# First FFN of a hybrid decoder layer: input sums on VectorE in their own buffers, block weights fetched from the outset, plain weights in program order

## The chip, the cores and the metric

The kernel runs on one core of a Trainium2 chip. The metric is the device time of one execution in microseconds; a quoted time is the median of several executions. One more execution was taken with the hardware profiler, and every row of a trace comes from that one. In the rows PE is TensorE's matmul stream, DVE is VectorE, ACT is ScalarE, POOL is GpSimd, and SP is SyncE, which here issues DMAs and nothing else.

## The reference

One layer: a SwiGLU half step and a norm, three token mixers merged through gates, a second SwiGLU half step. The change concerns the first SwiGLU's input product.

```python
def swiglu_ffn(x, w_in, w_out):
    a, u = jnp.split(x @ w_in, 2, axis=-1)
    return (jax.nn.silu(a) * u) @ w_out

x = layer_norm(DEEPNORM_ALPHA * x + 0.5 * swiglu_ffn(x, ffn1_w_in[l], ffn1_w_out[l]), ln1_g[l], ln1_b[l])
mix = hybrid_mixer(x, mem, w_in[l], t5_table, ...)
x = layer_norm(DEEPNORM_ALPHA * x + mix, ln2_g[l], ln2_b[l])
x = layer_norm(DEEPNORM_ALPHA * x + 0.5 * swiglu_ffn(x, ffn2_w_in[l], ffn2_w_out[l]), ln3_g[l], ln3_b[l])
```

There are 512 tokens, 1024 channels and 2816 hidden units, all in float32.

## The kernel before

**Precision.** A float32 operand is split into a high part, rounded to the matmul's own float32 type by ScalarE (line 57), and a low part, the remainder, made by VectorE (line 58, a `tensor_tensor` with two inputs in SBUF). A product of two operands is three matmuls: high by high, low by high, high by low (`mm3`, lines 76 to 78). So a weight tile is usable when its DMA, then ScalarE, then VectorE have done their part, and the third matmul of the three is the one that needs VectorE's.

**The first FFN.** The hidden units are worked through in 22 blocks `j` of 128, each with two weight slabs of 128x1024, one for `a`, one for `u`. `gate` (line 128) takes SiLU of the first product on ScalarE (line 130) and multiplies by the second on VectorE (line 131). Blocks 0 to 2 are *plain*: 48 matmuls of 512 columns each, 144 in all. Blocks 3 to 21 are *seven-product* blocks: `x` is cut into four quarters (256 tokens by 512 channels), four sums of quarters `s1` to `s4` are split once and for all, and every block then needs seven quarter products of 12 matmuls of 256 columns (line 204), with the weights' own sums made on VectorE (lines 189 to 193).

**The opening.** `bring` (line 358) fetches `x` in five pieces and splits it; `first` calls it between the pieces of block 0's weights (line 150), and block 0's matmuls go channel block by channel block, `k` 0 to 7. `x` lands in `raws`, which take the two buffers `kv0` and `kv1`. The same two buffers hold the raw weights of the seven-product blocks (`s_raw`, line 176, DMAs of lines 177 and 178), so these can't be fetched until the sums are finished. `x_sums` (line 105) makes the four sums in place on GpSimd (lines 109 to 112) and splits them.

**What sets the order.** The scheduler places instructions of equal priority as they are written; everything under `tc.high_priority()` is placed ahead. Before, block 0's fetch, all plain weights (`weight`, line 65) and all block weights stand under it. There are three raw weight buffers (`w_raw`), which a later tile takes when the former has been split. All DMAs are issued by SP in one order, and a DMA that has to wait for a buffer holds up those behind it. The completion of a DMA is signalled on one of eight semaphores used in turn; in the listings they stand as DMAHW0 to DMAHW7, and an issue that reuses one waits for the transfer that had it.

Of the kernel before, what the change touches and what calls it, by code (L numbers as in the profile page):

```python
# [42 lines left out]
def hybrid_layer(ctx: ExitStack, tc: tile.TileContext, a: dict, out: bass.AP):  # L43
# [72 lines left out]
    def sum_tiles(pool):  # L116

        made = {n: [pool.tile([P, 4, 256], F32R, tag=f"s{n}{x}", name=f"s{n}{x}") for x in "hl"] for n in (3, 2, 1, 4)}
        return [made[n] for n in (1, 2, 3, 4)]

    def ffn_in(xT, w_in, gpool, kvp, pool, plain, sums=None, first=None, then=None):

# [14 lines left out]

        done = 0
        if first is not None:
            po = [ps("mm"), ps("mm")]  # L140
            with tc.high_priority():
                w = [weight_tiles() for _ in range(2)]
                steps = ((0, 1), (1, 2), (2, 4), (4, 6), (6, 8))
                for k0, k1 in steps:
                    c = slice(k0 * P, k1 * P)
                    r = slice((k0 % 4) * P, (k0 % 4 + k1 - k0) * P)
                    first(k0, k1)
                    for n in range(2):
                        raw, hi, lo = w[n]
                        nc.sync.dma_start(raw[:, c], slab(w_in, 0, n)[k0 // 4][:, r])  # L150
                        split(hi[:, c], lo[:, c], raw[:, c])
# [4 lines left out]
            then()
            done = 1
        else:
            opened = [([ps("mm"), ps("mm")], [weight(*slab(w_in, j, n)) for n in range(2)]) for j in range(2)]
# [729 lines left out]
```

## Time and profile before

| | |
|---|---|
| median of 3 runs | 1264.58 us (1264.14 to 1264.92) |
| the profiled execution | 1264.7 us, of which the span from first to last instruction is 1262.9 us |
| PE busy | 1241.3 us, 98% of the span |
| VectorE busy | 715.6 us, 57% |
| ScalarE busy | 474.1 us, 38% |
| GpSimd busy | 106.6 us, 8% |
| mean granted TensorE clock | 0.996 |

PE is the engine that sets the time: where it doesn't start a matmul, or starts them at half the rate, the program gets longer by that much. So the reading looks for the stretches where PE waits or runs slowly, and for what ended each wait.

### The profile page before, as it was taken

The numbers are of one execution on the slowest core, as the hardware profiler recorded it, in microseconds if no ns is written. First come the engines' busy times: TensorE is split into PE (matmuls) and PEld (weight loads), VectorE is DVE, ScalarE is ACT, GpSimd is POOL, SyncE is SP. The second block draws the span as 40 slices with busy tenths as digits, with TensorE's granted clock in tenths as the row PEclk, the third lists the DMA queues.
The fourth block names the chain that finished last, engine by engine and source line by source line (L and its number), as shares of the span: only waits on it lengthen the run. The fifth ranks groups of instructions, "written<-read, shape, count | busy, mean of one in ns | idle before, by whom it ended". The sixth has DMA issues, their size and how long they took to land.

```text
span 1262.9 us, 16539 instructions
## 1 busy us (share of the span) xinstructions
PE 1241.3 (98%) x6499; PEld 1053.2 (83%) x6499; DVE 715.6 (57%) x1146; ACT 474.1 (38%) x748; POOL 106.6 (8%) x91
## 2 busy tenths in 40 slices
PE   7999999999999999999999999999999999999997
PEld 5899999988888887788877877888988888888886
DVE  6788888643396899972554544435732222223336
ACT  5355555532235533523444532321332222222221
POOL 3000000000000000010321331120000000000003
PEclk9999999999999999999999999999999999999999
DMA  5333334543357233223333233233433322335312
GB/s 168 119 115 101 101 101 134 164 170 100 100 174 247 70 100 92 90 70 115 100 94 99 76 100 124 93 100 117 137 114 100 100 95 91 99 100 166 89 45 100
DMA packets 50926, 141.24 MB, mean 112 GB/s; under 512 B 6008, under 2 KB 7416, under 8 KB 50848
## 3 DMA queue, kind: packets, MB, share of 16 engines
q1 hardware_dynamic: 50848, 140.18, 34.8%
q8 instruction: 51, 0.84, 0.3%
q14 instruction: 27, 0.22, 0.1%
HBM read 132.80 MB, written 8.93 MB: 112 GB/s over the span
## 4 chain that ended last, share of the span: by engine, by line
PE 84%; DVE 9%; DMA 3%; issue 1%; ACT 1%; POOL 1%; SPq 0%; DVEq 0%; POOLq 0%; ACTq 0%
PE ps_mm L76 13%; PE ps_mm L77 13%; PE ps_mm L78 13%; PE ps_mm L204 8%; PE ps_ax L204 6%; PE ps_mm L251 4%; PE ps_mm L250 4%; PE ps_mm L249 4%; PE ps_ax L251 3%; PE ps_ax L250 3%; PE ps_ax L249 3%; DVE w_lo L58 2%; DMA w_raw<-in_ffn_w_in 1%; DVE mask L557 1%; PE ps_mm L350 1%
## 5 line engine op out<-in xcount | busy, mean ns | idle before, releaser
L58 DVE TENSOR_TENSOR w_lo<-w_raw,w_hi 128x1024 fp32r<-128x1024 f32 (+2 forms) x187 | 229.0, 1229 | 212.7 <-ACT w_hi L57 209.9
L57 ACT CAST w_hi<-w_raw 128x1024 fp32r<-128x1024 f32 (+2 forms) x187 | 188.5, 1013 | 367.2 <-PE ps_mm L77 297.8
L76 PE MATMUL ps_mm<-xh,w_hi 128*128 128x512 f32 (+2 forms) x824 | 315.6, 384 | 5.6 <-ACT w_hi L57 5.6
L78 PE MATMUL ps_mm<-xh,w_lo 128*128 128x512 f32 (+2 forms) x824 | 315.3, 383 | 3.8 <-DVE w_lo L58 3.8
L77 PE MATMUL ps_mm<-xl,w_hi 128*128 128x512 f32 (+2 forms) x824 | 315.7, 383 | 0.0
L76 PEld LDWEIGHTS ps_mm<-xh,w_hi 128*128 128x128 f32 x824 | 156.1, 190 | 34.8 <-ACT w_hi L57 6.5
L78 PEld LDWEIGHTS ps_mm<-xh,w_lo 128*128 128x128 f32 x824 | 156.6, 190 | 33.7 <-DVE w_lo L58 4.7
L77 PEld LDWEIGHTS ps_mm<-xl,w_hi 128*128 128x128 f32 x824 | 156.6, 190 | 28.3
L58 DVE TENSOR_TENSOR g_kv<-g,g_kv 128x512 fp32r<-128x512 f32 x36 | 24.7, 691 | 89.5 <-ACT g_kv L57 89.5
L302 POOL TENSOR_TENSOR mv<-mv,minus_half 128x1 f32<-128x1 f32 x12 | 10.0, 835 | 734.3 <-DVE mv L301 734.2
L57 ACT CAST g_kv<-g 128x512 fp32r<-128x512 f32 x36 | 22.2, 623 | 105.7 <-PE ps_ax L250 105.7
L131 DVE TENSOR_TENSOR g<-sa,ps_mm 128x512 f32<-128x512 f32 x25 | 17.2, 687 | 71.8 <-PE ps_mm L78 71.8
L249 PE MATMUL ps_ax<-w_hi,g_kv 128*128 128x512 f32 x144 | 56.2, 390 | 0.0
L251 PE MATMUL ps_ax<-w_hi,g_kv 128*128 128x512 f32 x144 | 56.1, 390 | 0.0
L249 PE MATMUL ps_mm<-w_hi,g_kv 128*128 128x512 f32 x144 | 56.1, 389 | 0.0
L251 PE MATMUL ps_mm<-w_hi,g_kv 128*128 128x512 f32 x144 | 56.0, 389 | 0.0
L250 PE MATMUL ps_mm<-w_lo,g_kv 128*128 128x512 f32 x144 | 56.0, 389 | 0.0
L250 PE MATMUL ps_ax<-w_lo,g_kv 128*128 128x512 f32 x144 | 56.0, 389 | 0.0
L57 ACT CAST s_hi<-s_raw 128x1024 fp32r<-128x1024 f32 x38 | 39.8, 1048 | 42.8 <-PE ps_ax L204 15.4
L58 DVE TENSOR_TENSOR s_lo<-s_raw,s_hi 128x1024 fp32r<-128x1024 f32 x38 | 46.5, 1225 | 9.9 <-ACT s_hi L57 9.9
L726 POOL TENSOR_TENSOR bt<-strip,mask 128x128 f32<-128x128 f32 (+3 forms) x32 | 39.8, 1256 | 127.2 <-DVE dst L731 113.1
L204 PE MATMUL ps_ax<-xh,s_hi 128*128 128x256 f32 x152 | 43.1, 284 | 0.3 <-DVE g L232 0.3
(261 smaller groups left out, 2415.0 us busy)
## 6 DMA issues: line engine op xcount, KB each, us to landing
w_raw<-in_ffn_w_in SPq DMA_DIRECT2D x96, 256.0 KB, 3.3
w_raw<-in_ffn_w_out SPq DMA_DIRECT2D x44, 512.0 KB, 3.6
s_raw<-in_ffn_w_in SPq DMA_DIRECT2D x38, 512.0 KB, 4.6
w_raw<-in_w_gate SPq DMA_DIRECT2D x24, 512.0 KB, 3.6
w_raw<-in_w_br SPq DMA_DIRECT2D x12, 512.0 KB, 3.5
y<-z SPq DMA_DIRECT2D x16, 256.0 KB, 2.4
res<-y SPq DMA_DIRECT2D x8, 512.0 KB, 4.3
w_raw<-in_w_out SPq DMA_DIRECT2D x8, 512.0 KB, 3.5
```

The source lines that it names most:

```text
L57: nc.scalar.copy(hi, src)
L58: nc.vector.tensor_tensor(lo, src, hi.bitcast(F32), op=ALU.subtract)
L76: nc.tensor.matmul(po, wh, xh, start=first, stop=False)
L77: nc.tensor.matmul(po, wh, xl, start=False, stop=False)
L78: nc.tensor.matmul(po, wl, xh, start=False, stop=last)
L131: nc.vector.tensor_tensor(g[j], sa, po[1], op=ALU.mult)
L204: nc.tensor.matmul(po, wn[:, cols(k)], xn[:, k], start=first and k == n == 0, stop=k == 3 and n == 2, skip_group_check=not first)
L249: nc.tensor.matmul(po, lh[:, c], wh[:, half(h)], start=j == 0, stop=False)
L250: nc.tensor.matmul(po, lh[:, c], wl[:, half(h)], start=False, stop=False)
L251: nc.tensor.matmul(po, ll[:, c], wh[:, half(h)], start=False, stop=j == n - 1)
L350: nc.tensor.matmul(po[t], xl, wh[:, half(kk)], start=False, stop=k == KT - 1)
L726: nc.gpsimd.tensor_tensor(bt[:, :n], strip[h][:, S - n:], masks[i], op=ALU.add)
```

## The change

1. `x` is fetched by quarters into four tiles of their own (tag `quarter`, nine buffers of 128x4x256) instead of `kv0` and `kv1`: two DMAs for a piece in place of one, and two splits, one for each half of the tokens.
2. `x_sums` makes the four sums with VectorE instead of GpSimd, each followed by its split into two further `quarter` tiles. It is called after block 1's gate, not after block 0's.
3. Plain weights of the first FFN are fetched without raised priority (`early` is false), so they keep the place that the program gives them: block 0 first, then block 1, then block 2.
4. The raw weights of the first two seven-product blocks go without raised priority too; `kv0` and `kv1` are free from the start.
5. A slab is one DMA of 512 KB instead of two of 256 KB, in both FFNs; since its two halves are then stored in another order, `at` rotates the channel blocks for `n` = 1.

```diff
-    def weight(*parts):
-
-        with tc.high_priority():
+    def weight(src, early=True):
+
+        with tc.high_priority() if early else nullcontext():
             raw, hi, lo = weight_tiles()
-            n = 1024 // len(parts)
-            for i, src in enumerate(parts):
-                nc.sync.dma_start(raw[:, i * n:(i + 1) * n], src)
+            nc.sync.dma_start(raw, src)
             split(hi, lo, raw)
         return hi, lo
...
     def slab(w, j, n):
 
-        return [block(w, j, b) for b in ((B11, B21) if n == 0 else (B12, B22))]
+        return w[j][:, 1024 * (1 - n):1024 * (2 - n)]
+
+    def at(n, k):
+
+        return cols(k if n == 0 else (k + 4) % KT)
...
-    def x_sums(raw, sums):
-
-
-        (a11, a21), (a12, a22) = [[r[:, :, 256 * t:256 * t + 256] for t in range(2)] for r in raw]
-        nc.gpsimd.tensor_tensor(a22, a21, a22, op=ALU.add)
-        nc.gpsimd.tensor_tensor(a21, a11, a21, op=ALU.subtract)
-        nc.gpsimd.tensor_tensor(a11, a22, a11, op=ALU.subtract)
-        nc.gpsimd.tensor_tensor(a12, a12, a11, op=ALU.subtract)
-        for (hi, lo), src in zip(sums, (a22, a11, a21, a12)):
-            split(hi, lo, src)
...
+    def x_sums(raw, new):
+
+
+        a22, a21, a11, a12 = raw
+        made = []
+        for dst, x, y, op in ((a22, a21, a22, ALU.add), (a21, a11, a21, ALU.subtract),
+                              (a11, a22, a11, ALU.subtract), (a12, a12, a11, ALU.subtract)):
+            nc.vector.tensor_tensor(dst, x, y, op=op)
+            made.append((new(), new()))
+            split(*made[-1], dst)
+        s1, s3, s2, s4 = made
+        return s1, s2, s3, s4
...
         if first is not None:
             po = [ps("mm"), ps("mm")]
-            with tc.high_priority():
-                w = [weight_tiles() for _ in range(2)]
...
+            w = [weight_tiles() for _ in range(2)]
+            for k0, k1 in ((0, 1), (1, 2), (2, 4), (4, 6), (6, 8)):
+                first(k0, k1)
+                for n in range(2):
+                    raw, hi, lo = w[n]
+                    c = slice(at(n, k0).start, at(n, k1 - 1).stop)
+                    nc.sync.dma_start(raw[:, c], slab(w_in, 0, n)[:, c])
+                    split(hi[:, c], lo[:, c], raw[:, c])
...
             gate(0, po)
-            then()
             done = 1
...
             for n in range(2):
-                product(po[n], weight(*slab(w_in, j, n)), slice(0, S))
+                product(po[n], n, weight(slab(w_in, j, n), first is None), slice(0, S))
             gate(j, po)
+            if j == 1:
+                s1, s2, s3, s4 = sums()
 
         def weights(j):
 
-            with tc.high_priority():
+            with tc.high_priority() if j > plain + 1 else nullcontext():
...
-            raws = [kvp.tile([P, 4, S], F32, tag=f"kv{q}", name=f"x_raw{q}") for q in range(2)]
-            sums = sum_tiles(pool)
+            def quarter_tile(dtype=F32R):
+                return pool.tile([P, 4, 256], dtype, tag="quarter", name="quarter", bufs=9)
+
+            a22, a21, a11, a12 = raws = [quarter_tile(F32) for _ in range(4)]
 
             def bring(k0, k1):
-                raw = raws[k0 // 4][:, k0 % 4:k0 % 4 + k1 - k0]
-                nc.sync.dma_start(raw, a["xT"][:, k0:k1])
-                for k in range(k0, k1):
-                    split(xT[0][:, k], xT[1][:, k], raw[:, k - k0])
+                for t, raw in enumerate((a11, a21) if k0 < 4 else (a12, a22)):
+                    raw, ts = raw[:, k0 % 4:k0 % 4 + k1 - k0], slice(256 * t, 256 * t + 256)
+                    nc.sync.dma_start(raw, a["xT"][:, k0:k1, ts])
+                    split(xT[0][:, k0:k1, ts], xT[1][:, k0:k1, ts], raw)
```

Behind block 4 or so the two programs' instructions stand in the same order on every engine. What differs stands at three places. Line numbers in the listings of the changed kernel are its own.

SP, from the program's start, before (w_raw_122 and w_raw_125 are block 0's slabs, w_raw_244 and w_raw_275 block 1's):

```order
L360 DMA x_raw0_88<-in_xT 128x512
L150 DMA w_raw_122<-in_ffn1_w_in 128x128
L150 DMA w_raw_125<-in_ffn1_w_in 128x128
L71 DMA w_raw_244<-in_ffn1_w_in 128x512 x2
L360 DMA x_raw0_88<-in_xT 128x512
L150 DMA w_raw_122<-in_ffn1_w_in 128x128
L150 DMA w_raw_125<-in_ffn1_w_in 128x128
L360 DMA x_raw0_88<-in_xT 128x1024 [waits DMAHW0_49]
L150 DMA w_raw_122<-in_ffn1_w_in 128x256 [waits DMAHW1_49]
L150 DMA w_raw_125<-in_ffn1_w_in 128x256 [waits DMAHW2_49]
L71 DMA w_raw_275<-in_ffn1_w_in 128x512 [waits DMAHW4_49,DMAHW3_49,DVE_49]
```

and now (quarter_88 to quarter_91 are the four quarters of x, w_raw_116 and w_raw_119 block 0's slabs):

```order
L353 DMA quarter_90<-in_xT 128x256
L353 DMA quarter_89<-in_xT 128x256
L140 DMA w_raw_116<-in_ffn1_w_in 128x128
L140 DMA w_raw_119<-in_ffn1_w_in 128x128
L353 DMA quarter_90<-in_xT 128x256
L353 DMA quarter_89<-in_xT 128x256
L140 DMA w_raw_116<-in_ffn1_w_in 128x128
L140 DMA w_raw_119<-in_ffn1_w_in 128x128
L353 DMA quarter_90<-in_xT 128x2x256 [waits DMAHW0_49]
L353 DMA quarter_89<-in_xT 128x2x256 [waits DMAHW1_49]
L140 DMA w_raw_116<-in_ffn1_w_in 128x256 [waits DMAHW2_49]
L140 DMA w_raw_119<-in_ffn1_w_in 128x256 [waits DMAHW3_49]
```

Block 1's slabs have left the opening, and x comes in twice as many pieces, no issue of which waits for another engine.

SP, behind the last piece of block 0, before (w_raw_342 is block 2's second slab, s_raw_376 and s_raw_472 are the seven-product blocks 3 and 4):

```order
L365 DMA ident_78<-in_ident 128x128 [waits DMAHW5_49]
L366 DMA gncol_79<-in_gncol 128x8 [waits DMAHW6_49]
L71 DMA w_raw_342<-in_ffn1_w_in 128x512 [waits DMAHW2_49,DMAHW7_49,DMAHW1_49,DVE_49]
L71 DMA w_raw_342<-in_ffn1_w_in 128x512 [waits DMAHW0_49]
L177 DMA s_raw_472<-in_ffn1_w_in 128x1024 [waits DVE_49,Activation_49,Pool_49]
L177 DMA s_raw_376<-in_ffn1_w_in 128x1024 [waits DVE_49]
L178 DMA s_raw_376<-in_ffn1_w_in 128x1024 [waits DMAHW3_49]
L178 DMA s_raw_472<-in_ffn1_w_in 128x1024 [waits DMAHW4_49]
```

and now (w_raw_235 and w_raw_265 are block 1's slabs, w_raw_320 and w_raw_350 block 2's, s_raw_383 and s_raw_479 blocks 3 and 4):

```order
L140 DMA w_raw_116<-in_ffn1_w_in 128x256 [waits DMAHW2_49]
L140 DMA w_raw_119<-in_ffn1_w_in 128x256 [waits DMAHW3_49]
L69 DMA w_raw_235<-in_ffn1_w_in 128x1024 [waits DMAHW4_49]
L168 DMA s_raw_383<-in_ffn1_w_in 128x1024 [waits DMAHW5_49]
L69 DMA w_raw_265<-in_ffn1_w_in 128x1024 [waits DMAHW6_49,DMAHW2_49,DVE_49]
L69 DMA w_raw_320<-in_ffn1_w_in 128x1024 [waits DMAHW7_49,DMAHW3_49,DVE_49]
L169 DMA s_raw_383<-in_ffn1_w_in 128x1024 [waits DMAHW0_49]
L69 DMA w_raw_350<-in_ffn1_w_in 128x1024 [waits DMAHW1_49,DMAHW4_49,DVE_49,Activation_49]
L168 DMA s_raw_479<-in_ffn1_w_in 128x1024
L169 DMA s_raw_479<-in_ffn1_w_in 128x1024
```

The two halves of s_raw_383 now stand among the plain slabs, and no block weight of these two waits for a sum of x.

DVE, around the end of block 0, before (w_lo_124 and w_lo_127 are the last low parts of block 0, w_lo_344 is block 2's second slab, g0 and g1 are the gates' products):

```order
L58 TENSOR_TENSOR xl_73<-x_raw1_89,xh_72 128x512 [waits DMAHW0_49,Activation_49]
L58 TENSOR_TENSOR xl_73<-x_raw1_89,xh_72 128x512 [waits Activation_49]
L58 TENSOR_TENSOR w_lo_313<-w_raw_311,w_hi_312 128x1024 [waits DMAHW2_49,DMAHW1_49,Activation_49]
L58 TENSOR_TENSOR w_lo_124<-w_raw_122,w_hi_123 128x256 [waits DMAHW3_49,Activation_49]
L58 TENSOR_TENSOR w_lo_127<-w_raw_125,w_hi_126 128x256 [waits DMAHW4_49,Activation_49]
L58 TENSOR_TENSOR s1l_95<-x_raw1_89,s1h_94 128x1024 [waits Activation_49]
L58 TENSOR_TENSOR s3l_91<-x_raw0_88,s3h_90 128x1024 [waits Activation_49]
L131 TENSOR_TENSOR g0_98<-sa_227,ps_mm_121 128x512 [waits PE_49,Activation_49]
L58 TENSOR_TENSOR s2l_93<-x_raw0_88,s2h_92 128x1024 [waits Pool_49]
L58 TENSOR_TENSOR s4l_97<-x_raw1_89,s4h_96 128x1024 [waits Activation_49]
L58 TENSOR_TENSOR w_lo_344<-w_raw_342,w_hi_343 128x1024 [waits DMAHW7_49,DMAHW0_49,Activation_49]
```

and now (quarter_88, 89 and 90, written by line 108, are sums; quarter_300 and quarter_305 low parts of sums; w_lo_237 and w_lo_267 block 1's slabs):

```order
L58 TENSOR_TENSOR w_lo_118<-w_raw_116,w_hi_117 128x256 [waits DMAHW2_49,Activation_49]
L58 TENSOR_TENSOR w_lo_121<-w_raw_119,w_hi_120 128x256 [waits DMAHW3_49,Activation_49]
L108 TENSOR_TENSOR quarter_88<-quarter_89,quarter_88 128x1024 [waits DVE_49]
L108 TENSOR_TENSOR quarter_89<-quarter_90,quarter_89 128x1024 [waits DVE_49]
L124 TENSOR_TENSOR g0_92<-sa_230,ps_mm_115 128x512 [waits PE_49,Activation_49]
L58 TENSOR_TENSOR w_lo_237<-w_raw_235,w_hi_236 128x1024 [waits DMAHW4_49]
L58 TENSOR_TENSOR quarter_300<-quarter_88,quarter_299 128x1024 [waits Activation_49]
L58 TENSOR_TENSOR w_lo_267<-w_raw_265,w_hi_266 128x1024 [waits DMAHW6_49,Activation_49]
L58 TENSOR_TENSOR quarter_305<-quarter_89,quarter_304 128x1024 [waits Activation_49]
L108 TENSOR_TENSOR quarter_90<-quarter_88,quarter_90 128x1024
L58 TENSOR_TENSOR w_lo_322<-w_raw_320,w_hi_321 128x1024 [waits DMAHW7_49,Activation_49]
L108 TENSOR_TENSOR quarter_91<-quarter_91,quarter_90 128x1024 [waits DVE_49]
```

Two sums and block 0's gate now stand ahead of block 1's first low part, which before had been made before block 0 was done; the other sums stand between the later slabs.

## Rows read from the trace of the kernel before

**Rows 1.** Windows: busy us (x count) by engine, PEclk granted clock, DMA share, GB/s.

```profile
4.00:14.00 10.00, 8.43 (x20) 6.15 (x21) 5.20 (x11) 4.28 (x11) 0.00 (x0) 1.00 0.73 232
24.00:34.00 10.00, 6.28 (x15) 4.68 (x16) 10.00 (x6) 5.21 (x6) 6.48 (x3) 0.67 0.17 54
62.00:1258.00 1196.00, 1190.10 (x6270) 1011.23 (x6268) 671.55 (x1094) 445.77 (x704) 95.60 (x83) 1.00 0.35 110
```

**Rows 2.** Timeline of PE to 62 us: start us, duration us, instruction, [idle before <-releaser].

```profile
4.42 1.22 PE L76 MATMUL ps_mm<-xh,w_hi 128*128 128x512 f32 x2 [4.42 <-ACT w_hi L57]
...
8.50 0.80 PE L76 MATMUL ps_mm<-xh,w_hi 128*128 128x512 f32 x1 [1.15 <-ACT w_hi L57]
...
13.75 0.40 PE L76 MATMUL ps_mm<-xh,w_hi 128*128 128x512 f32 x1
...
25.96 0.50 PE L78 MATMUL ps_mm<-xh,w_lo 128*128 128x512 f32 x1 [2.06 <-DVE w_lo L58]
...
28.45 0.79 PE L78 MATMUL ps_mm<-xh,w_lo 128*128 128x512 f32 x1 [1.76 <-DVE w_lo L58]
...
34.17 0.40 PE L78 MATMUL ps_mm<-xh,w_lo 128*128 128x512 f32 x1
...
49.36 0.28 PE L204 MATMUL ps_mm<-xh,s_hi 128*128 128x256 f32 x1
...
52.90 0.39 PE L204 MATMUL ps_mm<-s2h,s_hi 128*128 128x256 f32 x1 [0.50 <-ACT c L212]
...
59.46 0.39 PE L204 MATMUL ps_mm<-s4h,s_hi 128*128 128x256 f32 x1 [0.54 <-ACT u L212]
```

**Rows 3.** Groups by shape, VectorE, first 19 us: xcount | busy us, mean ns | idle.

```profile
L58 DVE TENSOR_TENSOR w_lo<-w_raw,w_hi 128x1024 fp32r<-128x1024 f32 x2 | 2.4, 1224 | 6.1 <-ACT w_hi L57 6.1
L58 DVE TENSOR_TENSOR w_lo<-w_raw,w_hi 128x256 fp32r<-128x256 f32 x4 | 1.5, 421 | 0.0
```

**Rows 4.** Groups by shape, VectorE, 19 to 37 us.

```profile
L58 DVE TENSOR_TENSOR w_lo<-w_raw,w_hi 128x256 fp32r<-128x256 f32 x2 | 5.1, 2570 | 0.0
L58 DVE TENSOR_TENSOR s1l<-x_raw,s1h 128x1024 fp32r<-128x1024 f32 x1 | 3.4, 3393 | 0.0
...
L131 DVE TENSOR_TENSOR g<-sa,ps_mm 128x512 f32<-128x512 f32 x1 | 0.7, 675 | 0.0
```

**Rows 5.** Timeline of GpSimd, its four sums of x.

```profile
19.93 2.41 POOL L109 TENSOR_TENSOR x_raw<-x_raw,x_raw 128x1024 f32<-128x1024 f32 x1 [19.49 <-DVE xl L58]
...
28.20 2.44 POOL L112 TENSOR_TENSOR x_raw<-x_raw,x_raw 128x1024 f32<-128x1024 f32 x1
```

**Rows 6.** Timeline of SP's issues (the second number is the issue's length).

```profile
1.17 0.90 SPq L150 DMA_DIRECT2D w_raw<-in_ffn_w_in  x2
...
4.96 0.91 SPq L150 DMA_DIRECT2D w_raw<-in_ffn_w_in  x2
9.73 0.80 SPq L71 DMA_DIRECT2D w_raw<-in_ffn_w_in  x2
```

**Rows 7.** Windows while the first pieces come in, and a later one.

```profile
2.00:10.00 8.00, 4.43 (x10) 3.00 (x11) 2.62 (x5) 3.47 (x10) 0.00 (x0) 1.00 0.78 256
14.00:16.00 2.00, 2.00 (x10) 1.68 (x9) 0.46 (x1) 1.38 (x2) 0.00 (x0) 1.00 1.03 387
```

**Rows 8.** DMA issues of the first 60 us: xcount, KB each, median us to landing.

```profile
x_raw<-in_xT SPq DMA_DIRECT2D x3, 512.0 KB, 5.2
...
gncol<-in_gncol SPq DMA_DIRECT2D x1, 4.0 KB, 2.6
```

**Rows 9.** Groups by shape, ScalarE, first 34 us.

```profile
L57 ACT CAST w_hi<-w_raw 128x256 fp32r<-128x256 f32 x6 | 2.1, 401 | 0.0
...
L130 ACT ACTIVATE sa<-ps_mm 128x512 f32<-128x512 f32 x2 | 1.2, 597 | 1.0 <-PE ps_mm L78 0.9
```

**Rows 10.** Waits of the first 62 us: us in total, times, longest us.

```profile
ACT s_hi L57 <- DMA s_raw<-in_ffn_w_in: 10.2, 1, 10.2
```

More of the change, by code (lines that the diff above doesn't have):

```diff
@@ L1 @@
 import math
-from contextlib import ExitStack
+from contextlib import ExitStack, nullcontext
 import numpy as np
@@ L88, in new_xT, with ffn_in @@
                 xpool.tile([P, KT, S], F32R, tag="xl", name="xl"))
-    B22, B12, B11, B21 = range(4)
-    def block(w, j, n):
-        return w[j][:, half(n)]
     def slab(w, j, n):
-        return [block(w, j, b) for b in ((B11, B21) if n == 0 else (B12, B22))]
+        return w[j][:, 1024 * (1 - n):1024 * (2 - n)]
+    def at(n, k):
+        return cols(k if n == 0 else (k + 4) % KT)
     def quarter(xs, t, q):
         return [x[:, 4 * q:4 * q + 4, 256 * t:256 * t + 256] for x in xs]
-    def x_sums(raw, sums):
-        (a11, a21), (a12, a22) = [[r[:, :, 256 * t:256 * t + 256] for t in range(2)] for r in raw]
-        nc.gpsimd.tensor_tensor(a22, a21, a22, op=ALU.add)
-        nc.gpsimd.tensor_tensor(a21, a11, a21, op=ALU.subtract)
-        nc.gpsimd.tensor_tensor(a11, a22, a11, op=ALU.subtract)
-        nc.gpsimd.tensor_tensor(a12, a12, a11, op=ALU.subtract)
-        for (hi, lo), src in zip(sums, (a22, a11, a21, a12)):
-            split(hi, lo, src)
[L116 to L121, printed above, removed]
+    def x_sums(raw, new):
[8 more added lines that the diff above has]
+        return s1, s2, s3, s4
+    def ffn_in(xT, w_in, gpool, kvp, pool, plain, first=None, sums=None):
         xh, xl = xT
@@ L131, in gate, with product @@
             nc.vector.tensor_tensor(g[j], sa, po[1], op=ALU.mult)
-        def product(po, w, ts):
+        def product(po, n, w, ts):
             for k in range(KT):
-                mm3(po[:, ts], w[0][:, cols(k)], w[1][:, cols(k)], xh[:, k, ts], xl[:, k, ts],
+                mm3(po[:, ts], w[0][:, at(n, k)], w[1][:, at(n, k)], xh[:, k, ts], xl[:, k, ts],
                     k == 0, k == KT - 1)
@@ L140, in ffn_in @@
             po = [ps("mm"), ps("mm")]
-            with tc.high_priority():
-                w = [weight_tiles() for _ in range(2)]
[L143 to L151, printed above, removed]
+            w = [weight_tiles() for _ in range(2)]
[6 more added lines that the diff above has]
+                    split(hi[:, c], lo[:, c], raw[:, c])
             for k in range(KT):
                 for n in range(2):
-                    mm3(po[n], w[n][1][:, cols(k)], w[n][2][:, cols(k)], xh[:, k], xl[:, k], k == 0, k == KT - 1)
+                    mm3(po[n], w[n][1][:, at(n, k)], w[n][2][:, at(n, k)], xh[:, k], xl[:, k], k == 0, k == KT - 1)
             gate(0, po)
-            then()
             done = 1
         else:
-            opened = [([ps("mm"), ps("mm")], [weight(*slab(w_in, j, n)) for n in range(2)]) for j in range(2)]
+            opened = [([ps("mm"), ps("mm")], [weight(slab(w_in, j, n)) for n in range(2)]) for j in range(2)]
             for ts in (slice(0, 256), slice(256, 512)):
@@ L162, in ffn_in @@
                     for n in range(2):
-                        product(po[n], w[n], ts)
+                        product(po[n], n, w[n], ts)
             for j, (po, w) in enumerate(opened):
```

3 lines of the change are left out of this document (1 added, 2 removed).

## The prediction

> **What bounds the kernel now.** I read the windows first. From 62 us to 1258 us PE is busy 1190.1 of 1196 us, at full granted clock, through 6270 matmuls [rows 1]: nothing there can be won or lost by a change that leaves the order of that part alone, and behind the opening the order is unchanged. The same view shows two poor stretches, both in the opening: 4 to 14 us, with 20 matmuls in 10 us, and 24 to 34 us, with 15 matmuls, VectorE busy for all of the 10 us and the clock at 0.67 [rows 1]. The timeline of PE says what they cost [rows 2]. The 144 matmuls of the plain blocks run from 4.42 to 49.36 us. Between 34.17 and 49.36 there are 67 of them without a gap: 15.19 / 67 = 0.227 us each, the full rate. At this rate 144 take 32.6 us; they took 44.9, so 12.3 us are lost, and they can be placed:
>
> - 4.42 to 13.75 us: 18 matmuls (6 up to the break of 1.15 us, 12 behind it) in 9.33 us, against 18 x 0.227 = 4.1. Lost 5.2. The 12 behind the break take 5.25 us, 0.44 each, the level of 1.2 GHz.
> - 13.75 to 23.90 us (where the wait of 2.06 us begins): full rate, nothing lost.
> - 23.90 to 28.45 us: two matmuls, between waits of 2.06 and 1.76 us for VectorE's low parts. Lost 4.55 - 0.45 = 4.1.
> - 28.45 to 34.17 us: 13 matmuls in 5.72 us, again 0.44 each, since the clock had fallen during these waits. Lost 5.72 - 2.95 = 2.8.
>
> The sum is 12.1, so 0.2 is left over. In the seven-product part PE then waits 0.50 and 0.54 us for ScalarE's copies [rows 2].
>
> Why was VectorE late at 24 us? Its low parts of 128x256 take 0.42 us each in the first 19 us [rows 3] and 2.57 us each between 19 and 37 us; one of 128x1024 takes 3.39 us, against 1.22 [rows 3, 4]. In just this time GpSimd makes the four sums, from 19.93 to 30.64 us [rows 5]. Each of the slow VectorE operations holds on until a sum has ended. So the third and fourth items, 6.9 us, belong to the sums on GpSimd.
>
> **The change part by part.** *Sums to VectorE (gain 6.9).* The GpSimd work goes, and with it what holds VectorE up: both waits and the fall of the clock behind them. VectorE gets four operations more; their form, float32 128x1024 from two inputs in SBUF, is that of w_lo, 1.22 us [rows 3], together 4.9 us. Two stand ahead of block 0's gate and are done while PE still works on block 0. The others and the eight splits' halves stand between slabs needed 5 to 16 us later. On the path they cost nothing; if that cover were gone, one would cost 1.22.
>
> *A new wait (cost 1.6).* In VectorE's new order g0, block 0's gate, stands ahead of block 1's first low part w_lo_237. g0 waits for SiLU, and SiLU for the first of block 0's two sums, which ends three matmuls before the other. Let T be the end of block 0. SiLU takes 0.60 [rows 9] and is done close to T; g0 takes 0.68 [rows 4], starts when the last sum is out, some 0.15 after T, and w_lo_237 needs 1.22 more: T + 2.05. PE has two matmuls (0.45) before it needs this. It waits 1.6 us. Behind w_lo_237 on VectorE stand the sums' splits and w_lo_267, needed 5.4 us later. Bounds: 0, if g0 were early, and 2.8 more than 1.6 if the clock falls again, the price of the 13 slow matmuls above.
>
> *The opening without block 1 (gain 2.4).* Before, SP issued 512 KB of block 1 between the first and the second piece of x, and then sat idle from 5.87 to 9.73 us, waiting for a raw buffer [rows 6]. Now it issues the 20 pieces of x and block 0 in a row, two in 0.90 us [rows 6], say 0.47 each with the pause between, none waiting for an engine. By bytes: 2.10 MB of x and 1.05 MB of weights. From 2 to 10 us, with pieces of just such sizes, 256 GB/s came in [rows 7]: 3.15 MB / 256 GB/s = 12.3 us, so the last lands at about 14.3. Earliest: the last issue ends at 0.7 + 20 x 0.47 = 10.1, and 4 KB landed 2.6 after their issue [rows 8]: 12.7; 387 GB/s, the best window [rows 7], is no tighter. Latest: 17.5, worked out below. One k needs 384 KB, 1.5 us at 256 GB/s, while its six matmuls take 2.6 us at the low clock: once started, PE should not run dry before the clock is up. I take the start at 4.55 (x now takes two issues, 0.1 later), 12 slow matmuls without a break, 5.25 us as in the row, and 36 at full rate, 8.2: T = 18.0. The last pieces, landed at 14.3, split on ScalarE and VectorE by 15.6 (two casts of 0.40, two low parts of 0.42 behind [rows 3, 9]), are needed at 15.3 for the last twelve matmuls. I add 0.3: T = 18.3. At full rate from 4.42 it would be 15.3, so 3.0 are lost where 5.2 were; with the unplaced 0.2 gone the gain is 2.4.
>
> Here stands a rule against the change. The Trainium skill (DMA: Bandwidth & Descriptors, section Bandwidth) says to batch transfers to 1 MiB or more for three quarters of the peak, and measures 138 GB/s for one of 64 KB; the change halves the pieces of x. By that figure alone 3.15 MB would take 23 us, an estimate from the page, T would be near 28 and the time near 1266. The row speaks against it: 256 GB/s with such pieces, because several are in flight.
>
> *Block weights from the outset, own buffers (gain 0.9).* Before, ScalarE waited 10.2 us for the first s_raw [rows 10], whose buffer the sums still held, and the two waits of PE in the seven-product part follow from the work that then came in one heap. Now s_raw_383 is issued right behind block 1's first slab, 20 us earlier. I take 0.9 of the 1.04.
>
> *Plain weights in turn, one DMA of 512 KB.* w_raw_265 is issued when a buffer of block 0 is split, 15.6, behind 1 MB in flight: landed at 15.6 + 5.2 [rows 8] = 20.8; needed at T + 1.6 + 5.4 = 25.3. w_raw_350 waits for w_lo_237, 20.4, lands at 25.6, is needed at 36. Nothing. In the second FFN PE waits for no weight within 62 to 1258 us, so halving the issues there gives nothing either.
>
> **Sum.** 6.9 + 2.4 + 0.9 - 1.6 = 8.6 us. The profiled execution took 1264.7 (span 1262.9); 1256.1. It stands 0.1 above the median, so 1256.0.
>
> **The rivals.** *The clock falls at the new wait*, or rises later: one more low stretch costs 2.8 (28.45 to 34.17) and gives 1258.8. For it: before, it fell after PE had stood still for 3.8 us around two matmuls. Against it: here one wait of 1.6 us between unbroken runs. Chance 0.18.
>
> *Small pieces come in late.* Eight landing semaphores are used in turn. If every landing took 5.2 us, the longest median [rows 8], the 17th issue would wait for two rounds and the last would be issued at 12.3 and land at 17.5. The last twelve matmuls then start at 18.4: T = 21.1, 1258.8. Chance 0.14. The page's rule on small transfers would show up in this way.
>
> *Slower than before: the clock never comes up in the plain blocks 0 and 1.* If waits for pieces break PE's run again and again, as the break at 7.35 us did before, block 0's 36 fast matmuls stay at 0.44 instead of 0.227 (7.7 us), and if the wait at T starts this anew, block 1's 48 as well (10.2): 1256.0 + 17.9 = 1273.9. It decides from 40 more slow matmuls on (8.6 / 0.213). Against it: 1.5 us of transfer for 2.6 us of slow matmuls. Chance 0.04.
>
> *It doesn't do what it says:* 512 KB of block weights ahead of plain slabs make these late, and the gain goes into waits for them. w_raw_265 has 4.5 us of slack; to eat the gain it would have to land 13 us later than worked out. 1264.7. Chance 0.05.
>
> *Better than forecast:* g0 early, no wait at T, last pieces early: 1256.0 - 1.6 - 0.3 = 1254.1. Chance 0.07.
>
> **How the numbers follow.** The forecast has 0.52. The two rivals that are still faster have 0.32, no gain 0.05, slower 0.04, better 0.07. The range runs from 1254.0 to 1260.6: the better case, and above the clock or the pieces, and two thirds of both together (1261.6). A measurement can tell about 0.2% here, 2.5 us: faster, below 1262.0, 0.90; same 0.06; slower 0.04.
>
> **What would show it.** Right: no VectorE low part over 1.3 us in the opening; block 0 ends at 18 to 19 us; one wait of about 1.6 us for w_lo behind it; the granted clock at 1.0 from about 10 us on; the first 256-column matmul at about 41.8 us; no wait over 0.3 us behind it. Wrong: a granted clock of 0.5 after block 0; waits for w_hi in block 0 that end with a landing of x; waits of PE for w_raw_265's slab; any difference behind 62 us that isn't a shift.

## The result and the profile after

The changed kernel takes 1255.44 us (median of 4 runs, 1254.87 to 1256.19), the kernel before beside it 1264.55 us: a ratio of 0.9928, 95% interval 0.9911 to 0.9946. So it is faster by 9.1 us (medians); the two profiled executions differ by 8.5 us of span (1262.9 and 1254.4; the profiled execution of the changed kernel, 1256.19, is the longest of its four). The forecast was 1256.0.

The windows of the changed kernel, in the stretches of [rows 1] and behind block 0:

```profile
4.00:14.00 10.00, 9.54 (x27) 6.95 (x28) 6.19 (x15) 5.92 (x15) 0.00 (x0) 1.00 0.89 278
14.00:24.00 10.00, 8.47 (x37) 6.63 (x37) 9.28 (x12) 7.20 (x10) 0.00 (x0) 1.00 0.86 294
24.00:34.00 10.00, 10.00 (x46) 8.29 (x45) 10.00 (x10) 4.38 (x5) 0.00 (x0) 1.00 0.37 127
62.00:1249.00 1187.00, 1181.48 (x6195) 1002.41 (x6193) 663.36 (x1083) 441.13 (x695) 95.38 (x83) 1.00 0.34 110
```

The stretch from 24 to 34 us, where before there were 15 matmuls at a clock of 0.67, now has 46 at 1.00, though VectorE is still busy for all of it. The 1.00 from 4 to 14 us can't be taken at its word, here or in [rows 1]: the first record of the clock in this trace is its rise at 10.7 us, and until 10.30 the matmuls start 0.43 us apart, the lower level (lines below, at the warm start). VectorE's groups by shape from 14 to 34 us, to be held against [rows 4]:

```profile
L108 DVE TENSOR_TENSOR quarter<-quarter 128x1024 f32<-128x1024 f32 x4 | 4.9, 1221 | 0.0
L58 DVE TENSOR_TENSOR w_lo<-w_raw,w_hi 128x1024 fp32r<-128x1024 f32 x4 | 4.9, 1220 | 0.0
L58 DVE TENSOR_TENSOR w_lo<-w_raw,w_hi 128x256 fp32r<-128x256 f32 x3 | 1.2, 420 | 0.0
```

The four sums (line 108) take 1.22 us each, and no low part is stretched. PE's timeline has one wait left in the plain blocks, where [rows 2] had three (1.15, 2.06 and 1.76 us):

```profile
4.46 0.80 PE L74 MATMUL ps_mm<-xh,w_hi 128*128 128x512 f32 x1 [4.46 <-ACT w_hi L57]
...
18.96 0.39 PE L74 MATMUL ps_mm<-xh,w_hi 128*128 128x512 f32 x1
...
21.11 0.50 PE L76 MATMUL ps_mm<-xh,w_lo 128*128 128x512 f32 x1 [1.53 <-DVE w_lo L58]
...
42.55 0.28 PE L194 MATMUL ps_mm<-xh,s_hi 128*128 128x256 f32 x1
...
231.46 0.40 PE L239 MATMUL ps_mm<-w_hi,g_kv 128*128 128x512 f32 x1
```

18.96 is the 49th matmul, the end of block 0; 42.55 the start of the seven-product part; 231.46 its end. In the trace of before these three are:

```profile
20.57 0.39 PE L76 MATMUL ps_mm<-xh,w_hi 128*128 128x512 f32 x1
...
240.15 0.40 PE L249 MATMUL ps_mm<-w_hi,g_kv 128*128 128x512 f32 x1
```

and 49.36 [rows 2]. From this the 8.5 us can be placed. The plain blocks took 44.94 us from their first matmul on, and take 38.09: 6.85 won. The seven-product part took 190.79, and takes 188.91: 1.88 won. The start moved by 0.04 and the rest of the program by 0.2, both to the worse. The landmarks "plain part" (first matmul to first 256-column matmul) and "seven-product part" (from there to the row at 231.46) are used for all runs below.

### The profile page after: what moved, and what is told of

It is laid out like the page before. It is cut to its first block, busy times and chain, and to the rows that moved or that the text cites. A ratio compares the mean times of both kernels' runs of the same rounds, so it can differ in the third digit from the quotient of the medians.

```text
span 1254.4 us, 16465 instructions
## 1 busy us (share of the span) xinstructions
PE 1237.5 (99%) x6499; PEld 1050.8 (84%) x6499; DVE 714.9 (57%) x1152; ACT 475.0 (38%) x750; POOL 96.2 (8%) x87
## 4 chain that ended last, share of the span: by engine, by line
PE 89%; DVE 7%; ACT 1%; DMA 1%; issue 1%; POOL 1%; DVEq 0%; SPq 0%; POOLq 0%; ACTq 0%
PE ps_mm L74 15%; PE ps_mm L75 14%; PE ps_mm L76 14%; PE ps_mm L194 9%; PE ps_ax L194 7%; PE ps_mm L241 4%; PE ps_mm L239 4%; PE ps_mm L240 4%; PE ps_ax L241 3%; PE ps_ax L239 3%; PE ps_ax L240 3%; DVE w_lo L58 2%; PE ps_mm L340 1%; PE ps_mm L339 1%; PE ps_mm L338 1%; DVE mask L549 1%
## 5 line engine op out<-in xcount | busy, mean ns | idle before, releaser
L58 DVE TENSOR_TENSOR w_lo<-w_raw,w_hi 128x1024 fp32r<-128x1024 f32 (+2 forms) x187 | 224.4, 1204 | 204.5 <-ACT w_hi L57 201.5
L194 PE MATMUL ps_mm<-quarter,s_hi 128*128 128x256 f32 x456 | 84.7, 283 | 0.0
L194 PEld LDWEIGHTS ps_mm<-quarter,s_hi 128*128 128x128 f32 x456 | 71.1, 192 | 0.6 <-ACT u L202 0.6
L194 PE MATMUL ps_mm<-quarter,s_lo 128*128 128x256 f32 x228 | 64.5, 283 | 0.0
```

The lines of the kernel that those rows point to most:

```text
L58: nc.vector.tensor_tensor(lo, src, hi.bitcast(F32), op=ALU.subtract)
L194: nc.tensor.matmul(po, wn[:, cols(k)], xn[:, k], start=first and k == n == 0, stop=k == 3 and n == 2, skip_group_check=not first)
```

## The experiments

Theory A: the gain is GpSimd's, whose sums kept VectorE from its low parts. Rival B: it is the order of the fetches. Rival C: it is the early block weights, for which x got buffers of its own. Each run was compared with runs of the kernel before on the same chip (medians 1264.55 to 1265.00). A cut in a code excerpt is marked by three dots.

| run | median us | ratio to before, 95% | plain part | seven-product part |
|---|---|---|---|---|
| before, profiled | | | 44.94 | 190.79 |
| changed kernel | 1255.44 | 0.9928 (0.9911 to 0.9946) | 38.09 | 188.91 |
| changed kernel again | 1255.73 | 0.9928 (0.9916 to 0.9941) | 38.17 | 189.02 |
| before, sums on VectorE | 1259.28 | 0.9955 (0.9942 to 0.9967) | 38.17 | 192.07 |
| changed, sums on GpSimd | 1261.72 | 0.9973 (0.9963 to 0.9982) | 45.12 | 188.63 |
| changed, order undone | 1255.35 | 0.9925 (0.9913 to 0.9938) | 38.28 | 189.02 |
| changed, x in kv0, kv1 | 1255.51 | 0.9925 (0.9912 to 0.9939) | 38.19 | 189.15 |
| idle GpSimd additions | 1264.26 | 0.9992 (0.9984 to 1.0001) | 47.46 | 189.16 |
| idle GpSimd memsets | 1255.53 | 0.9928 (0.9914 to 0.9941) | 38.67 | 188.68 |
| slab ahead of the gate | 1254.01 | 0.9912 (0.9898 to 0.9925) | 37.60 | 188.63 |
| warm start | 1255.45 | 0.9925 (0.9911 to 0.9939) | 37.74 | 188.82 |
| whole pieces, x in kv0, kv1 | 1254.44 | 0.9915 (0.9901 to 0.9928) | 35.83 | 189.72 |
| whole pieces, half in kv0 | 1254.45 | 0.9919 (0.9905 to 0.9932) | 36.17 | 188.91 |
| two DMAs a slab | 1255.65 | 0.9927 (0.9914 to 0.9939) | 37.82 | 188.95 |

**The sums alone.** The kernel before, one word changed in four lines:

```diff
-        nc.gpsimd.tensor_tensor(a22, a21, a22, op=ALU.add)
+        nc.vector.tensor_tensor(a22, a21, a22, op=ALU.add)
...
```

> The kernel before, with one edit: the four sums of x run on VectorE instead of GpSimd; order, buffers and DMAs of the opening stay. Theory A (the sums on GpSimd cost 6.9 us by holding up VectorE's low parts): no low part of 128x256 over 0.5 us, both waits of 2.06 and 1.76 us gone, no second stretch at the half clock, the plain blocks end at 42 to 43 us instead of 49.4. But x still lies in the two buffers of the block weights, which the sums' splits release at about 31 us; with 10 us from issue to landing in the trace of before, the first block weights land at about 41 and are usable at 43 to 45, so part of the 6.9 should come back as a wait of 1 to 4 us ahead of the first 256-column matmul: 1258.5 to 1262. Without such a wait 1257.6. Rival B (the order of the fetches is what held up the low parts): no change, 1264.5.

1259.28 us. The plain part falls to 38.17, as in the changed kernel: theory A explains all of this part, and B, taken net, none. (Of the 6.77 us won, 0.82 lie in block 0, which took 15.33 us from its first matmul to the 49th instead of 16.15; in this execution the clock rose at 7.6 us instead of 13.7.) But the seven-product part gets 1.3 us longer. PE's timeline there:

```profile
42.84 0.39 PE L204 MATMUL ps_mm<-xh,s_hi 128*128 128x256 f32 x1 [0.45 <-ACT s_hi L57]
...
44.17 0.39 PE L204 MATMUL ps_ax<-s3h,s_hi 128*128 128x256 f32 x1 [0.83 <-ACT s_hi L57]
...
49.44 0.39 PE L204 MATMUL ps_mm<-s2h,s_lo 128*128 128x256 f32 x1 [0.71 <-DVE s_lo L58]
```

This is the new wait that the expectation names: the buffers come free when the last sum is split, and the block weights come too late for a PE that is now 6.5 us earlier. VectorE's timeline shows both:

```profile
33.06 1.22 DVE L58 TENSOR_TENSOR s4l<-x_raw,s4h 128x1024 fp32r<-128x1024 f32 x1
41.81 1.23 DVE L189 TENSOR_TENSOR ts<-s_raw 128x1024 f32<-128x1024 f32 x1 [7.53 <-DMA s_raw<-in_ffn_w_in]
```

**The sums back on GpSimd.** The changed kernel, `nc.vector` back to `nc.gpsimd` in `x_sums`.

> The changed kernel, with one edit: the four sums go back to GpSimd; everything else as changed. Theory A: GpSimd makes the sums from about 16.7 to 27 us, and block 1's low parts (1.22 us each alone) take 2.4 to 3.4 us in this time; the wait at the end of block 0 grows from 1.5 to 2.5 to 4 us, and if the granted clock falls in it, another 2.8: 1257 to 1262. Rival B (order and buffers alone made the gain): 1255.4, since GpSimd is otherwise idle there.

1261.72 us. The whole 7.0 us of the plain part are gone again (the seven-product part keeps its gain, 188.63), in the way of [rows 2]: two waits for low parts, of 1.01 and 4.15 us, and half clock behind the second (matmuls 0.43 us apart, granted clock 0.66 from 24 to 34 us):

```profile
18.24 0.50 PE L76 MATMUL ps_mm<-xh,w_lo 128*128 128x512 f32 x1 [1.01 <-DVE w_lo L58]
...
24.87 0.80 PE L76 MATMUL ps_mm<-xh,w_lo 128*128 128x512 f32 x1 [4.15 <-DVE w_lo L58]
```

**GpSimd work that nobody waits for.** In the two runs above VectorE also waits for the sums' results. So the changed kernel got additions without a reader:

```diff
             gate(0, po)
+            spare = pool.tile([P, 2, S], F32, tag="spare", name="spare", bufs=1)
+            for _ in range(4):
+                nc.gpsimd.tensor_tensor(spare, xh[:, 6:8].bitcast(F32), xh[:, 6:8].bitcast(F32), op=ALU.add)
             done = 1
```

> The changed kernel with four GpSimd additions of 128x1024 in a buffer of their own added, which start when the last piece of xh is made (about 15 us) and whose result nobody reads. No instruction of another engine waits for them. Theory A (GpSimd and VectorE get in each other's way): VectorE's operations of 1.22 us take 2.4 to 3.4 us between 15 and 25 us, the wait behind block 0 grows from 1.5 to 3 to 5 us, perhaps with a fall of the clock: 1257 to 1262. Rival (what delayed the low parts was the waiting for the sums' results, an order of dependences): VectorE's operations keep 1.22 us and the time is 1255.4.

1264.26 us, the whole gain lost. VectorE's timeline, with GpSimd's behind it:

```profile
15.85 4.15 DVE L58 TENSOR_TENSOR w_lo<-w_raw,w_hi 128x256 fp32r<-128x256 f32 x2
19.92 5.74 DVE L108 TENSOR_TENSOR quarter<-quarter 128x1024 f32<-128x1024 f32 x2
25.59 0.67 DVE L124 TENSOR_TENSOR g<-sa,ps_mm 128x512 f32<-128x512 f32 x1
26.19 1.21 DVE L58 TENSOR_TENSOR w_lo<-w_raw,w_hi 128x1024 fp32r<-128x1024 f32 x1
```

```profile
15.29 9.30 POOL L148 TENSOR_TENSOR spare<-xh 128x1024 f32<-128x1024 f32 x4 [14.85 <-ACT xh L57]
```

The first two additions and the two low parts one by one:

```profile
15.29 2.40 POOL L148 TENSOR_TENSOR spare<-xh 128x1024 f32<-128x1024 f32 x1 [14.85 <-ACT xh L57]
15.85 2.12 DVE L58 TENSOR_TENSOR w_lo<-w_raw,w_hi 128x256 fp32r<-128x256 f32 x1
17.76 1.96 POOL L148 TENSOR_TENSOR spare<-xh 128x1024 f32<-128x1024 f32 x1
17.89 2.11 DVE L58 TENSOR_TENSOR w_lo<-w_raw,w_hi 128x256 fp32r<-128x256 f32 x1
```

Two low parts take 4.15 us instead of 0.76 and two sums 5.74 instead of 2.48, just while GpSimd adds; from 26 us on all is as always. No dependence joins the two engines here, so GpSimd stands in VectorE's way: each low part ends 0.28 us behind an addition (17.97 behind 17.69, 20.00 behind 19.72). In the kernel before it was the same: the low parts of 2.57 us [rows 4] ended 0.3 us behind the second and the third sum (25.91 behind 25.62, 28.40 behind 28.12).

**GpSimd writes only.** The same with memsets:

```diff
...
+            nc.scalar.copy(spare[:, 0, 0:8], xh[:, 6, 0:8].bitcast(F32))
+            for _ in range(10):
+                nc.gpsimd.memset(spare, 0.0)
```

> The run with idle GpSimd work, but with ten memsets of the same 128x1024 buffer in place of the four additions, so that GpSimd is busy at the same time and writes, but reads nothing; ScalarE copies eight columns into the buffer first, which starts the memsets at about 15 us. The additions stretched VectorE's two-input operations from 1.22 to 2.9 us and cost 8.8 us. If it is GpSimd's reads that stand in VectorE's way (the Trainium skill, SBUF — State Buffer, section Who interferes with whom, says that a VectorE operation with two inputs in SBUF contends with GpSimd's reads): VectorE's operations keep 1.22 us, 1255.4. Rival: any work of GpSimd on SBUF does it: operations of over 2 us on VectorE while the memsets run, 1257 or more.

1255.53 us, nothing lost. VectorE and GpSimd:

```profile
15.86 0.75 DVE L58 TENSOR_TENSOR w_lo<-w_raw,w_hi 128x256 fp32r<-128x256 f32 x2
16.53 2.47 DVE L108 TENSOR_TENSOR quarter<-quarter 128x1024 f32<-128x1024 f32 x2
```

```profile
14.75 10.07 POOL L149 MEMSET spare<- 128x1024 f32 x10 [14.32 <-ACT spare L147]
```

Ten microseconds of GpSimd work, and not one VectorE operation is longer. So neither a busy GpSimd nor its writes are enough; the additions do two things that the memsets don't, reading SBUF and adding, and no run here separates these. The Trainium skill (SBUF — State Buffer, section Who interferes with whom) says that a VectorE operation with both inputs in SBUF contends with a GpSimd operation that reads SBUF, not with one that only writes it, and that what they contend for is locked by one of them at a time. The two runs agree with both: 0.75 us beside the memsets against 4.15 beside the additions, and each held low part ends just behind an addition.

**The order undone.** The changed kernel, with block 0's fetch and the plain slabs under raised priority again:

```diff
+            with tc.high_priority():
+                for k0, k1 in ((0, 1), (1, 2), (2, 4), (4, 6), (6, 8)):
...
-                product(po[n], n, weight(slab(w_in, j, n), first is None), slice(0, S))
+                product(po[n], n, weight(slab(w_in, j, n)), slice(0, S))
```

> The changed kernel, with one edit: block 0's fetch and the plain slabs stand under raised priority again, so that block 1's first slab (512 KB) is issued between the first and the second piece of x; sums on VectorE, own buffers and early block weights stay. If the opening without block 1 is worth the 2.4 us of the prediction and the wait behind block 0 costs 1.5: block 0 starts with a break again and ends 2 to 3 us later, at 21 to 22 us, but the wait of 1.53 us goes, because block 1's low part is made before the gate: 1256 to 1257. Rival: the order is worth nothing by itself, 1254 (only the wait goes).

1255.35 us, between the two forecasts: the order is worth nothing by itself. Block 0 ends 1.6 us later (49th matmul at 20.51, as in the kernel before; 2 to 3 us were expected), and the wait behind it, 1.53 us, is gone; the two cancel.

```profile
8.63 0.80 PE L74 MATMUL ps_mm<-xh,w_hi 128*128 128x512 f32 x1 [1.62 <-ACT w_hi L57]
...
20.51 0.39 PE L74 MATMUL ps_mm<-xh,w_hi 128*128 128x512 f32 x1
```

**The buffers undone.** The changed kernel with x in the block weights' buffers:

```diff
-            a22, a21, a11, a12 = raws = [quarter_tile(F32) for _ in range(4)]
+            kv = [kvp.tile([P, 2, 4, 256], F32, tag=f"kv{q}", name=f"x_raw{q}") for q in range(2)]
+            a22, a21, a11, a12 = raws = [kv[1][:, 1], kv[0][:, 1], kv[0][:, 0], kv[1][:, 0]]
```

> The changed kernel, with one edit: the four quarters of x land in the two buffers that the raw block weights take (as before), so that these can only be fetched when the sums are split; sums on VectorE and the order of the plain slabs stay. If the own buffers are worth something: the first block weights are issued at about 30 us, land at 35 to 40, and the seven-product part waits 0 to 3 us: 1256 to 1258.5. If the prediction's 0.9 us is all: 1256.3. Rival: nothing is waited for, since the first block weights are needed only at 42.5 us: 1255.4.

1255.51 us: the buffers are worth nothing by themselves either. Here the sums are done earlier than in the run with the sums alone, and the block weights with them:

```profile
30.45 1.22 DVE L58 TENSOR_TENSOR quarter<-x_raw,quarter 128x1024 fp32r<-128x1024 f32 x1
...
38.05 2.36 DVE L180 TENSOR_TENSOR ts<-s_raw 128x1024 f32<-128x1024 f32 x2 [5.09 <-DMA s_raw<-in_ffn_w_in]
```

So of the last 3.8 us (1259.28 to 1255.44), either edit, order or buffers, is enough beside the smaller edits that both runs keep (x in quarters, no raised priority for the first block weights, each sum written beside its split, one DMA a slab): with the new order (and each sum written beside its split) the sums end 2.6 us sooner (33.06 and 30.45) and the first block weights are there at 38.05 instead of 41.81; with own buffers the sums don't matter for them. The parts don't add up to the whole. What the smaller edits bring of it is not shown, but for the one DMA, which is undone below.

**The wait behind block 0.** The changed kernel, block 1's first slab written ahead of `gate(0, po)`:

```diff
+            ahead = [weight(slab(w_in, 1, 0), False)]
             gate(0, po)
```

> The changed kernel, with block 1's first slab written ahead of block 0's gate, so that on VectorE its low part stands before g0 instead of behind it. If the wait of 1.53 us is g0's doing, as the prediction says: the low part is made right behind the two sums, which end at about 18.6 us, so at 19.8; PE needs it 0.45 us after the end of block 0 (18.96), and the wait falls to about 0.4 us: 1254.2. Rival: the wait is the DMA's or ScalarE's (w_hi ready at 17.6 us), then it stays and the time is 1255.4.

1254.01 us, 1.4 less than the changed kernel, and none of its runs (1253.55 to 1254.38) reaches one of those. In the two traces the plain part is only 0.5 us shorter, because block 0 took 15.17 us in this execution and 14.50 in the other. The wait:

```profile
20.21 0.50 PE L76 MATMUL ps_mm<-xh,w_lo 128*128 128x512 f32 x1 [0.37 <-DVE w_lo L58]
```

1.53 has become 0.37 us: it was g0's place in VectorE's order.

**A warm start, and the same kernel twice.** Seven matmuls on a zeroed tile ahead of block 0:

```diff
...
+            for _ in range(7):
+                nc.tensor.matmul(idle, warm[:, 0:P].bitcast(F32R), warm.bitcast(F32R), start=True, stop=True)
```

> The changed kernel with seven matmuls of 128x512 on a zeroed tile, whose result nobody reads, before block 0's first, so that PE is at work from about 1.5 us on instead of 4.46. Theory: block 0 is bound by its last pieces, which land at 15 us; the granted clock rises some us earlier, PE then waits for pieces, block 0 ends at 18.3 to 19 us as now: 1254.8 to 1255.4. Rival: the 14 slow matmuls are the loss (14 x 0.2 = 2.8 us), and with the clock up early block 0 ends at about 16.2 us: 1252.6 to 1253.5.

1255.45 us, no gain. Then the changed kernel once more:

> The changed kernel once more, for a second trace. In the traces so far the granted clock rose between 7.0 and 13.7 us, in kernels whose first six matmuls are alike. If the kernel sets that moment, it rises at about 10.7 us again; if it is different from one execution to the next, it rises elsewhere in this trace and the time is still 1255.4 within 0.6, since block 0 then waits for its last pieces.

1255.73 us. Three traces of the opening, first the changed kernel's, where matmuls stand 0.43 us apart (1.2 GHz) until 10.30 and 0.23 behind it:

```profile
9.32 0.63 PE L76 MATMUL ps_mm<-xh,w_lo 128*128 128x512 f32 x1
9.74 0.76 PE L74 MATMUL ps_mm<-xh,w_hi 128*128 128x512 f32 x1
10.30 0.56 PE L75 MATMUL ps_mm<-xl,w_hi 128*128 128x512 f32 x1
10.70 0.39 PE L74 MATMUL ps_mm<-xh,w_hi 128*128 128x512 f32 x1
...
13.05 0.50 PE L74 MATMUL ps_mm<-xh,w_hi 128*128 128x512 f32 x1
```

the second trace of the same kernel:

```profile
6.79 0.51 PE L74 MATMUL ps_mm<-xh,w_hi 128*128 128x512 f32 x1
7.15 0.40 PE L75 MATMUL ps_mm<-xl,w_hi 128*128 128x512 f32 x1
7.38 0.40 PE L76 MATMUL ps_mm<-xh,w_lo 128*128 128x512 f32 x1
...
9.90 0.50 PE L74 MATMUL ps_mm<-xh,w_hi 128*128 128x512 f32 x1 [1.43 <-ACT w_hi L57]
...
18.65 0.39 PE L74 MATMUL ps_mm<-xh,w_hi 128*128 128x512 f32 x1
```

and the warm start:

```profile
1.48 3.35 PE L138 MATMUL ps_ax<-warm 128*128 128x512 f32 x7 [1.48 <-DVE warm L135]
...
5.91 0.51 PE L74 MATMUL ps_mm<-xh,w_hi 128*128 128x512 f32 x1
6.26 0.39 PE L75 MATMUL ps_mm<-xl,w_hi 128*128 128x512 f32 x1
...
9.24 0.50 PE L74 MATMUL ps_mm<-xh,w_hi 128*128 128x512 f32 x1 [0.97 <-ACT w_hi L57]
...
18.78 0.39 PE L74 MATMUL ps_mm<-xh,w_hi 128*128 128x512 f32 x1
```

The clock rises at 10.7, 7.0 and 6.1 us, and the 13th matmul (9.74, 9.90, 9.24) and the end of block 0 (18.96, 18.65, 18.78) stand nearly still: where the clock is up early, PE waits for the third channel block instead. In the new order block 0 is bound by its pieces, not by the clock, and by the third and the fourth, not by the last: the 25th matmul (13.05 in the first trace) is the first of the fourth piece, and waited for its weights, the first of these two casts, which ended at 13.00:

```profile
12.60 0.71 ACT L57 CAST w_hi<-w_raw 128x256 fp32r<-128x256 f32 x2
```

The 37th (16.24), the first of the last piece, follows the matmul before it at full rate. In the old order the clock does count: block 0 took 16.15, 16.43 and 15.33 us (kernel before, order undone, sums alone), with the rise at 13.7, 12.8 and 7.6.

**Whole pieces of x.** The kernel with x in kv0 and kv1, one DMA for a piece (15 issues instead of 20):

```diff
...
-                    nc.sync.dma_start(raw, a["xT"][:, k0:k1, ts])
+                nc.sync.dma_start(kv[k0 // 4][:, k0 % 4:k0 % 4 + k1 - k0], a["xT"][:, k0:k1])
```

> The kernel of the run with x in the two block weight buffers, and each piece of x in one DMA again (15 issues for x and block 0 instead of 20), split by halves as now. It prices the small pieces. If smaller pieces bring less in a microsecond: the last pieces land 1 to 2 us before 15 us and block 0 ends 0.5 to 1.5 us earlier: 1254 to 1255. If bytes are what counts (the prediction's way): they land at the same time, 1255.5. In this kernel block 1's first low part stands ahead of g0 on VectorE, which may take another 1 us off the wait behind block 0.

1254.44 us; the plain part is 35.83, the shortest of all. It isn't the pieces: block 0 ends at 18.73, as with small ones (it began at 4.66). The last pieces do come earlier (ScalarE casts block 0's last weights at 14.28 us, against 15.08), but the third channel block comes later (the 13th matmul waits until 10.35). What went is the wait behind block 0, as the scheduler now placed block 1's first low part at 16.91 us, ahead of g0:

```profile
16.91 1.22 DVE L58 TENSOR_TENSOR w_lo<-w_raw,w_hi 128x1024 fp32r<-128x1024 f32 x1
18.11 1.23 DVE L58 TENSOR_TENSOR quarter<-x_raw,quarter 128x1024 fp32r<-128x1024 f32 x1
19.25 0.68 DVE L124 TENSOR_TENSOR g<-sa,ps_mm 128x512 f32<-128x512 f32 x1
```

0.8 us goes back in the seven-product part (a wait of 0.57 us at 62.27). With the second half of x in a buffer of its own:

> The kernel with whole pieces of x, but only the first half of x lies in a block weight buffer; the second half has a buffer of its own (and the sums eight instead of nine), so that the first block weights are fetched from the outset again. With whole pieces the plain blocks took 35.8 us against 38.1 in the changed kernel, while the seven-product part took 0.8 us longer, with a wait of 0.57 us at 62 us. If that wait came from the late block weights, it goes here: 1253.4 to 1253.9. Rival: the block weights, now in flight beside the plain slabs, delay these, or the wait has another cause: 1254.4 or more.

that wait is gone and the seven-product part is 188.91 again. The profiled execution is the shortest of all (span 1252.0), but the median, 1254.45 (1253.77 to 1255.19), is no better than the run above: which of the last two and the slab ahead of the gate is best can't be told from these runs.

**Two DMAs a slab.**

> The changed kernel with every slab in two DMAs of 256 KB again, in both FFNs. The prediction counted the merging at nothing: 1255.4, no other waits. Rival: SP's longer chain of issues or the smaller transfers cost something at the plain slabs: 1255.7 to 1257.

1255.65 us, and the wait of 1.53 us as its only one behind the opening: merging is worth nothing, as the prediction had it.

## Why the prediction was right, step by step

- *Sums to VectorE, 6.9.* Right in cause, and nearly in size: 6.8 by the run with the sums alone (44.94 to 38.17), 7.0 back with the sums on GpSimd (38.09 to 45.12). Behind block 0 alone, from the 49th matmul to the first 256-column one, 28.79 us became 22.84, of which 0.45 are the new wait for block weights: 6.4.
- *The new wait, 1.6.* 1.53, at the place named, and g0 is shown to be its cause.
- *The opening, 2.4.* The step that failed in kind. Block 0 ended at 18.96, not 18.3. From the first matmul to the 49th it took 14.50 us, where it had taken 16.15: 1.65 won, not 2.4, and the first 256-column matmul stood at 42.55 instead of 41.8. Against the other two traces of the old order, 16.43 and 15.33, the gain is 1.9 and 0.8. The prediction counted slow matmuls and let PE never run dry before the clock was up. The first 12 did take 5.28 us, as forecast; the 36 behind them took 9.22 instead of 8.2, as two more were slow (9.74 to 10.70) and the fourth piece came just too late (starts 0.29 to 0.42 us apart from 12.76 to 14.15). In the next execution seven were slow instead of 14, and PE stood still for 1.43 us, for weights that ScalarE could cast only when the third piece of x had landed. That is one of the prediction's own signs of being wrong; the time came out the same. The last pieces, for which the prediction added 0.3, were not waited for.
- *Opening and wait together* were to bring 0.8; the run with the order undone puts them at 0.1 to 0.2 by the plain part (38.28 against 38.17 and 38.09), and at nothing by the medians.
- *Block weights, 0.9.* Mis-sized: 1.88. The prediction took two waits of PE (0.50 and 0.54); a third of 0.35 us stood at 61.5 us (1.39 together), and a matmul behind a wait took 0.39 us instead of 0.28 [rows 2], by which 0.33 more is explained, an estimate; 0.16 is left open. It also put the gain on the own buffers alone; the run with x back in kv0 and kv1 kept it (189.15), as did those with the old order (189.02), with the sums on GpSimd (188.63) and with two DMAs a slab (188.95). So no single one of these is its cause; which of the edits together are is not shown.
- *Plain weights in turn and one DMA, 0.* Right: no wait of PE for them, ScalarE's casts of the two late slabs start at 20.57 and 26.33 us (forecast landings 20.8 and 25.6), and 1255.65 with two DMAs.

The sum, 8.6, met the 8.5 of the two traces partly by luck: the opening was taken 0.8 too high and the block weights 1.0 too low.

Of the rivals, the clock did not fall at the new wait (1.00 from 14 to 24 us), small pieces cost the end of block 0 no more than 0.3 us (18.96 and 18.65 against 18.73 and 18.85 with whole pieces), and neither slower case came. The Trainium skill's figure for one 64 KB transfer (DMA: Bandwidth & Descriptors, section Bandwidth), measured there on transfers issued from GpSimd, did not decide here, where SP issues them. In the changed kernel's windows 225 GB/s came in from 2 to 10 us, less than the 256 that the prediction took, and 349 from 10 to 14:

```profile
2.00:10.00 8.00, 5.54 (x13) 4.10 (x13) 4.06 (x11) 4.60 (x14) 0.00 (x0) 1.00 0.77 225
10.00:14.00 4.00, 4.00 (x15) 2.85 (x15) 2.69 (x6) 2.34 (x6) 0.00 (x0) 1.00 1.05 349
```

One sign named in the prediction was no sign: the clock, to be "at 1.0 from about 10 us on", rose at 10.7 us in one trace and at 7.0 in the next, with the same time.

## What to carry to other kernels

Where a low-share engine's operations suddenly take several times their usual length, look which engine is at work in just that time, and prove it with work that nobody waits for, then with work that reads nothing. A change of several edits is priced by undoing each one and by doing one alone: here two edits were each worth nothing when undone, while the run that lacks both, and some smaller ones, takes 3.8 us more. Before slow matmuls in an opening are counted as a loss, look whether the data would have been there for faster ones.

## What was not expected of the hardware

- The moment at which the granted clock rises differs from one execution of the same kernel to the next (10.7 and 7.0 us, from starts at 4.46 and 4.07 us); over all runs it lay between 6.1 and 13.7 us.
- The engine with the short operations paid most. Beside VectorE's work GpSimd's additions of 128x1024 took 1.96 to 2.76 us each where nobody waited for them, 2.85 on average as sums, and 2.41 to 3.21 in the kernel before (2.41 and 2.44 stand in [rows 5]); no run shows one by itself. VectorE's 128x256 low parts, each held until an addition was done, went from 0.42 to 2.1. Ten memsets took 1.0 us each and disturbed nobody.
- A wait of 1.53 us between unbroken runs of matmuls left the clock at 1.00 in every trace that had it (six). It fell in the kernel before, with waits of 2.06 and 1.76 us around two matmuls; in the run with idle additions, with waits of 0.88 and 1.06 us less than 1 us apart and again with one of 3.59; and in the run with the sums back on GpSimd, with one of 4.15.
